# A hybrid decoder trunk on one core: the MLP's last blocks in another order, and fewer mean matmuls at the end

## The chip, the cores and the metric

The kernel runs on one core of one Trainium2 chip, in one launch. The metric is the device time of that core in microseconds; the time before is the median of three runs.

## The reference

The program is a decoder trunk of four layers over 256 positions with 1024 features, all in float32. Each layer adds a token mixer, an MLP and a per-layer input embedding to the residual h; a norm ends the trunk. The mixers are a state-space layer (layers 0 and 3), forgetting attention (layer 1) and gated linear attention (layer 2). The change touches the MLP of all four layers and the final norm.

```python
def rmsnorm(x, g):
    y = x * rsqrt(mean(x * x, axis=-1) + 1e-6)
    return y * g

def sqrelu_mlp(xn, w1, w2):                 # w1: 1024 x 4096, w2: 4096 x 1024
    return square(relu(xn @ w1)) @ w2

for i in range(4):
    h = h + mixer_i(rmsnorm(h, norm_mix[i]))
    h = h + sqrelu_mlp(rmsnorm(h, norm_mlp[i]), mlp_w1[i], mlp_w2[i])
    h = h + (p[i] @ ple_proj[i]) * sigmoid(rmsnorm(h, norm_ple[i]) @ ple_gate[i])
return rmsnorm(h, final_norm)
```

## The kernel before

h lies in SBUF transposed, as eight tiles of 128 features x 256 positions (`H[k]`, in pairs `HH[n]`). Most weight products are done in split precision: a weight unit (256 rows x 512 columns, 512 KB) is loaded by the sync engine (L153, tile `raw`), rounded on ScalarE to its high part (L157, `whi`), and VectorE computes the remainder (L159, `wlo`). There are 3 buffers of `raw` and 4 each of `whi` and `wlo`, so units are made ready a few ahead of TensorE, and a buffer is free again when TensorE has done the last matmul that reads it. Activations have a high and a low part too, side by side.

The MLP is a sequence of steps, written out by hand in the string `MLP`. The 4096 hidden features are eight blocks of 512, 0 to 7.

- `fC` is the first product of block C: four weight units, each with 16 matmuls (`wide`, L209 and L211: for each of four output banks two of 512 columns with `whi` and two of 256 columns with `wlo`), 64 matmuls in all. Its evacuation (`summed`, L219 and L220: a copy on ScalarE and an add on VectorE for each bank, then the squared relu at L387 and a split at L267 and L268) makes the activation `s[C]`. A bank is free after its L220.
- `sCB` is the second product, from block C to half B of the outputs: two weight units, 32 matmuls. Four blocks accumulate in the same banks; after block 3 and after block 7 the sum `y` is evacuated (L219, L220), scaled (L406) and added to h (L408). For blocks 4 to 7 and half 1 a narrower form with two banks is used.

PSUM has eight banks in four tags: `acc` (3), `wk` (3), `po` (1), `mk` (1). `fC` uses three `wk` and `mk`, or three `acc` and `mk` for C = 4 and 5. `sC0` uses three `acc` and `po`; `sC1` three `wk` and `po` for blocks 0 to 3, and two `wk` for blocks 4 to 7. So in the part of the sequence that the change touches, s31 ends the sum y in `wk` and `po`, s40 begins a sum in `acc` and `po`, and f6 and f7 both use `wk` and `mk`.

Between the steps, after steps 1 to 15 of the sequence (counted from 0), `further()` runs one side step of a generator, `s5_ahead`, which prepares tables for layer 3's state-space mixer during the MLPs of layers 0 to 2. A side step's instructions are put behind the last weight load, the last `wlo` and the last matmul issued so far, each on its own engine. The fourteenth side step is a small table through the `mk` bank in layer 0 (L832 to L840), some small VectorE and ScalarE operations and loads in layer 1 (`bb`, `bc`, L708 to L710, L913, L914), and empty in layer 2; the fifteenth is empty in layer 0, a VectorE product of two factors in layer 1 (`rot`) and 34 small matmuls into `mk` in layer 2 (L922 to L927).

The final stage squares the eight tiles of h on ScalarE (L1167), sums each over the features by a matmul with a column of 1/1024 as the moving operand, for each half of the positions (L1169, into `ms`), and turns h to rows by matmuls with the gains on a diagonal (`turn`, L1163, into four banks). Each of these float32 matmuls shows as two instructions in the profile. The inverse root of the mean (L341 on VectorE, L345 on GpSimd) then scales the rows on VectorE (L1181) and ScalarE (L1183), and the sync engine writes them out (L1184). The last gate of layer 3 (L476 to L479) produces the last four tiles of h one by one.

The order of instructions on each engine is set ahead of time by a planner: it simulates the engines' time and takes, on each engine, the first instruction in program order that it holds to be ready. `issue_after(x)` puts the block's instructions on x's engine behind x. At run time each engine keeps the order that it was given.

Of the kernel before, what the change touches and what calls it, by code (L numbers as in the profile page):

```python
# [12 lines left out]
AF = mybir.ActivationFunctionType  # L13
ALU = mybir.AluOpType
# [15 lines left out]

MLP = "f0 f1 f2 s00 f3 s10 s20 s30 s01 s11 f4 s21 f5 s31 s40 f6 f7 s50 s60 s70 s41 s51 s61 s71"


def _turn():
# [22 lines left out]
class Trunk:  # L59
# [312 lines left out]
    def mlp(self, l):  # L372
# [41 lines left out]

        for i, step in enumerate(MLP.split()):
            c = int(step[1])
# [733 lines left out]
    def final(self, out):  # L1150
        nc = self.nc
        gain = self.t4("gain", (128, 8, 128))
        for k in range(8):
            nc.gpsimd.tensor_scalar(gain[:, k], self.ident, self.gains[:, 3 * DEPTH, k:k + 1], None, ALU.mult)
        ms = self.psum((128, 2))

        hT = [[self.psum((128, 4, 128), tag) for tag in tags] for tags in (("acc", "acc"), ("po", "mk"))]
        sq = [self.t4("sq", (128, 4, T), tag="c4") for _ in range(2)]
        halves = [slice(half * 128, (half + 1) * 128) for half in range(2)]

        def turn(k):
            for half, t in enumerate(halves):
                nc.tensor.matmul(hT[k // 4][half][:, k % 4], self.H[k][:, t], gain[:, k], start=True, stop=True)  # L1163

        for k in range(8):
            s = sq[k // 4][:, k % 4]
            nc.scalar.activation(s, self.H[k], AF.Square)  # L1167
            for half, t in enumerate(halves):
                last = nc.tensor.matmul(ms[:, half:half + 1], s[:, t], self.mean, start=k == half == 0, stop=k == 7, skip_group_check=True)  # L1169
            if k < 6:  # L1170
                turn(k)
        with self.tc.issue_after(last.ins):
            turn(6)
            turn(7)
        r = self.inverse_root(ms)
        for half in range(2):
            o = self.t4("fin", (128, 2, 512))
            for c in range(2):
                v, ps = o[:, c], hT[c][half].rearrange("t k f -> t (k f)")
                if c == 0:  # L1180
                    nc.vector.tensor_scalar(v, ps, r[:, half:half + 1], None, ALU.mult)  # L1181
                else:
                    nc.scalar.activation(v, ps, AF.Identity, scale=r[:, half:half + 1])  # L1183
            nc.sync.dma_start(out[half * 128:(half + 1) * 128, :], o.rearrange("t c f -> t (c f)"))  # L1184
# [62 lines left out]
```

## Time and profile before

| | |
|---|---|
| time, median of 3 runs | 1460.38 us (1458.03 to 1461.11) |
| profiled execution: time / span | 1461.99 us / 1460.2 us |
| TensorE (PE) busy | 1403.9 us, 96% |
| weight loads of TensorE (PEld) busy | 1266.9 us, 87% |
| VectorE (DVE) busy | 1054.3 us, 72% |
| ScalarE (ACT) busy | 723.2 us, 50% |
| GpSimd (POOL) busy | 86.8 us, 6% |
| mean granted TensorE clock | 0.984 |
| HBM read and written | 242.68 MB and 7.86 MB, 172 GB/s over the span |

A row of the timeline gives the start and length in us, the engine, the line of the kernel, the operation, output <- inputs, the shapes and how often it follows itself; in brackets stands how long the engine was idle before, and what ended that. A row of the waits gives an engine's operation, what it waited for, the sum in us, how often, and the longest. A row of the windows gives, for a stretch of the span, the busy time of each engine with the count of instructions, the granted clock (1.00 is full speed), the DMA engines' share and GB/s. Lengths of matmuls are modelled and overlap; their starts show the pace.

### The profile page before, as it was taken

Reading aid. Unit: us, or ns where it says so; the run is one execution under the profiler, and the core shown is the slowest. Engines: PE = TensorE matmul, PEld = TensorE weight load, DVE = VectorE, ACT = ScalarE, POOL = GpSimd, SP = SyncE. Lnnn points to the kernel's source line nnn. Section 1 sums busy time; section 2 is a strip of 40 time slices with the busy share of each in tenths; the row PEclk is TensorE's granted clock in tenths of the full one; section 3 lists DMA queues with packets and bytes.
Section 4 is the critical chain, followed back from the end, with each engine's and each line's share of the span. In section 5 each row is a group of like instructions: output and inputs, shape, how many; then the busy total and the mean of one; then the engine's idle time right before and its main releaser. Section 6 shows DMA issues by size and latency. Waiting matters only on the chain. (4 is left out here: it accounts for less than half of the span.)

```text
span 1460.2 us, 26622 instructions
## 1 busy us (share of the span) xinstructions
PE 1403.9 (96%) x10734; PEld 1266.9 (87%) x10734; DVE 1054.3 (72%) x1739; ACT 723.2 (50%) x1118; POOL 86.8 (6%) x142
## 2 busy tenths in 40 slices
PE   7889999999999999999999999999997899999998
PEld 6779988889999888888989588888997899888898
DVE  8994578767776578887676468886777946766665
ACT  3233565445655654545566455454563345545443
POOL 3100000010000000010004000100000000000020
PEclk9999999999999999999999999999999899999999
DMA  6623555566554347775555446774665446566551
GB/s 211 198 81 119 186 176 189 187 203 191 175 151 142 108 153 236 230 228 180 188 164 157 132 129 190 234 229 150 222 246 152 137 141 185 179 188 187 173 191 69
DMA packets 146347, 255.06 MB, mean 175 GB/s; under 512 B 24768, under 2 KB 35296, under 8 KB 146224
## 3 DMA queue, kind: packets, MB, share of 16 engines
q1 hardware_dynamic: 132912, 234.35, 50.8%
q0 software_dynamic: 5248, 17.31, 3.7%
q10 hardware_dynamic: 8064, 1.71, 0.6%
q8 instruction: 84, 1.38, 0.4%
q14 instruction: 39, 0.32, 0.1%
HBM read 242.68 MB, written 7.86 MB: 172 GB/s over the span
## 5 line engine op out<-in xcount | busy, mean ns | idle before, releaser
L159 DVE TENSOR_TENSOR wlo<-raw,whi 128x1024 fp32r<-128x1024 f32 x406 | 494.2, 1226 | 289.0 <-ACT whi L157 283.9
L157 ACT CAST whi<-raw 128x1024 fp32r<-128x1024 f32 x406 | 422.5, 1049 | 453.4 <-PE mk L209 77.7
L209 PE MATMUL wk<-x,whi 128*128 128x512 f32 x576 | 182.4, 401 | 7.5 <-DVE relu L220 7.5
L211 PEld LDWEIGHTS wk<-x,wlo 128*128 128x128 f32 x576 | 106.8, 190 | 23.1 <-issue 0.2
L209 PE MATMUL acc<-s,whi 128*128 128x512 f32 x384 | 118.5, 395 | 0.0
L211 PE MATMUL wk<-x,wlo 128*128 128x256 f32 x576 | 113.3, 281 | 0.0
L173 PE MATMUL acc<-x,whi 128*128 128x256 f32 x352 | 99.8, 288 | 4.6 <-DVE u L1060 2.9
L209 PEld LDWEIGHTS wk<-x,whi 128*128 128x128 f32 x576 | 92.2, 192 | 11.5 <-DVE relu L220 8.6
L174 PE MATMUL acc<-x,whi 128*128 128x256 f32 x352 | 100.3, 287 | 0.0
L175 PE MATMUL acc<-x,wlo 128*128 128x256 f32 x352 | 100.1, 286 | 0.0
L211 PEld LDWEIGHTS acc<-s,wlo 128*128 128x128 f32 x384 | 70.3, 188 | 15.8
L209 PE MATMUL mk<-x,whi 128*128 128x512 f32 x256 | 81.5, 395 | 0.0
L211 PE MATMUL acc<-s,wlo 128*128 128x256 f32 x384 | 74.3, 280 | 0.0
L173 PEld LDWEIGHTS acc<-x,whi 128*128 128x128 f32 x352 | 67.6, 194 | 6.4 <-issue 4.1
L175 PE MATMUL wk<-s,wlo 128*128 128x256 f32 x256 | 72.4, 283 | 0.0
L174 PE MATMUL wk<-s,whi 128*128 128x256 f32 x256 | 72.4, 283 | 0.0
L173 PE MATMUL wk<-s,whi 128*128 128x256 f32 x256 | 72.4, 283 | 0.0
L175 PEld LDWEIGHTS acc<-x,wlo 128*128 128x128 f32 x352 | 68.1, 194 | 0.1
L174 PEld LDWEIGHTS acc<-x,whi 128*128 128x128 f32 x352 | 68.0, 194 | 0.2
L209 PEld LDWEIGHTS acc<-s,whi 128*128 128x128 f32 x384 | 59.6, 189 | 1.4
L209 PE MATMUL po<-s,whi 128*128 128x512 f32 x192 | 60.7, 396 | 0.0
L209 PE MATMUL wk<-s,whi 128*128 128x512 f32 x192 | 60.1, 395 | 0.0
(399 smaller groups left out, 3376.0 us busy)
## 6 DMA issues: line engine op xcount, KB each, us to landing
raw<-mlp_w SPq DMA_DIRECT2D x256, 512.0 KB, 4.3
raw<-s_w_glu SPq DMA_DIRECT2D x32, 512.0 KB, 3.6
raw<-ple_gate SPq DMA_DIRECT2D x32, 512.0 KB, 3.6
raw<-fox_w_in SPq DMA_DIRECT2D x24, 512.0 KB, 3.8
raw<-gla_w_in SPq DMA_DIRECT2D x24, 512.0 KB, 3.6
raw<-s_w_out SPq DMA_DIRECT2D x16, 512.0 KB, 4.2
kept<-kept SPq DMA_DIRECT2D x12, 512.0 KB, 4.4
raw<-s_w_in SPq DMA_DIRECT2D x11, 512.0 KB, 4.7
```

Of the source, the lines that this page charges most:

```text
L157: nc.scalar.copy(hi, raw)
L159: self.last_lo = nc.vector.tensor_tensor(lo, raw, hi.bitcast(F32), ALU.subtract)
L173: mm(ps, hi, x[:, 0], start=first, stop=False, skip_group_check=True)
L174: mm(ps, hi, x[:, 1], start=False, stop=False, skip_group_check=True)
L175: self.last_mm = mm(ps, lo, x[:, 0], start=False, stop=last, skip_group_check=True)
L209: mm(ps[n], hi[:, i, s], v[i], start=first and i == 0, stop=False, skip_group_check=True)
L211: self.last_mm = mm(ps[n][:, 0], lo[:, i, s], v[i][:, 0], start=False, stop=last and i == UK - 1, skip_group_check=True)
```

## The change

In the MLP's sequence, f6 comes ahead of s40 instead of behind it. In the final stage, the squares of tiles 0 to 3 are added in pairs by one VectorE operation (tiles 0 and 1 with 2 and 3), so that two means instead of four are taken of them; the means of tiles 4 and 5 come behind those, their turns behind their means; the means of tiles 6 and 7 come behind the means of 4 and 5, and their turns behind their means. The means of the first four tiles and their turns are put behind the last matmul of the gate.

```diff
-MLP = "f0 f1 f2 s00 f3 s10 s20 s30 s01 s11 f4 s21 f5 s31 s40 f6 f7 s50 s60 s70 s41 s51 s61 s71"
+MLP = "f0 f1 f2 s00 f3 s10 s20 s30 s01 s11 f4 s21 f5 s31 f6 s40 f7 s50 s60 s70 s41 s51 s61 s71"
...
-        for k in range(8):
-            s = sq[k // 4][:, k % 4]
-            nc.scalar.activation(s, self.H[k], AF.Square)
+        def mean(x, first, last):
             for half, t in enumerate(halves):
-                last = nc.tensor.matmul(ms[:, half:half + 1], s[:, t], self.mean, start=k == half == 0, stop=k == 7, skip_group_check=True)
-            if k < 6:
+                self.last_mm = nc.tensor.matmul(ms[:, half:half + 1], x[:, t], self.mean, start=first and half == 0, stop=last, skip_group_check=True)
+
+        for k in range(4):
+            nc.scalar.activation(sq[0][:, k], self.H[k], AF.Square)
+        nc.vector.tensor_tensor(sq[0][:, 0:2], sq[0][:, 0:2], sq[0][:, 2:4], ALU.add)
+        with self.tc.issue_after(self.last_mm.ins):
+            for k in range(2):
+                mean(sq[0][:, k], k == 0, False)
+            for k in range(4):
                 turn(k)
-        with self.tc.issue_after(last.ins):
-            turn(6)
-            turn(7)
+        for k in range(4, 8):
+            nc.scalar.activation(sq[1][:, k - 4], self.H[k], AF.Square)
+        for k in range(4, 8, 2):
+            with self.tc.issue_after(self.last_mm.ins):
+                for i in range(2):
+                    mean(sq[1][:, k + i - 4], False, k + i == 7)
+            with self.tc.issue_after(self.last_mm.ins):
+                for i in range(2):
+                    turn(k + i)
```

## The prediction

> **What bounds the kernel now.** I read the page's busy times first, then TensorE's waits, then the timeline at the longest of them, then the windows with the granted clock, and last the chain of waits at the end.
>
> ```profile
> PE 1403.9 (96%) x10734; PEld 1266.9 (87%) x10734; DVE 1054.3 (72%) x1739; ACT 723.2 (50%) x1118; POOL 86.8 (6%) x142
> ```
> ```profile
> PE wk L209 <- DVE relu L220: 7.5, 6, 1.9
> ```
> ```profile
> 321.28 0.73 PE L209 MATMUL wk<-x,whi 128*128 128x512 f32 x2 [1.77 <-DVE relu L220]
> 659.76 0.73 PE L209 MATMUL wk<-x,whi 128*128 128x512 f32 x2 [1.94 <-DVE relu L220]
> 1007.58 0.73 PE L209 MATMUL wk<-x,whi 128*128 128x512 f32 x2 [1.20 <-DVE relu L220]
> 1371.17 0.73 PE L209 MATMUL wk<-x,whi 128*128 128x512 f32 x2 [1.39 <-DVE relu L220]
> ```
>
> TensorE is busy for 96%, so only its gaps can be won, or work taken off it. Its longest wait in sum is a first-product matmul waiting for L220, the VectorE add that frees a PSUM bank. Four of the six, 1.77 + 1.94 + 1.20 + 1.39 = 6.30 us, are one place, once in each layer: f7 starting directly behind f6 in the same banks (three wk and mk). The other two, 1.2 us, lie elsewhere in the MLPs and stay; they are what is late next.
>
> ```profile
> 1369.43 0.92 ACT L219 COPY relu<-wk 128x256 f32<-128x256 f32 x3
> ```
> ```profile
> 1369.55 1.23 DVE L159 TENSOR_TENSOR wlo<-raw,whi 128x1024 fp32r<-128x1024 f32 x1 [1.45 <-PE mk L209]
> 1370.70 1.08 DVE L220 TENSOR_TENSOR relu<-wk,relu 128x256 f32<-128x256 f32 x3
> ```
>
> In layer 3, f6's results leave PSUM only behind a weight remainder on VectorE: copied from 1369.43, the first add starts at 1370.70, and f7 at 1371.17.
>
> ```profile
> 319.30:322.67 3.37, 1.60 (x10) 1.22 (x10) 3.00 (x6) 2.48 (x6) 0.50 (x1) 1.00 0.91 208
> 322.67:326.08 3.41, 3.41 (x13) 2.92 (x12) 3.09 (x5) 1.22 (x2) 0.00 (x0) 0.50 1.03 327
> 321.28:334.10 12.82, 12.82 (x64) 11.15 (x65) 8.61 (x13) 6.44 (x9) 0.00 (x0) 0.87 0.73 234
> 657.20:660.59 3.39, 1.45 (x9) 1.12 (x8) 2.92 (x6) 2.95 (x6) 0.00 (x0) 1.00 0.47 171
> 660.59:664.00 3.41, 3.41 (x13) 2.83 (x12) 3.38 (x6) 1.24 (x2) 0.00 (x0) 0.50 0.69 206
> 659.76:672.60 12.84, 12.84 (x65) 11.11 (x66) 9.12 (x13) 5.60 (x10) 0.00 (x0) 0.87 0.38 123
> 1371.17:1382.45 11.28, 11.28 (x65) 9.86 (x65) 7.77 (x11) 5.49 (x10) 0.00 (x0) 1.00 0.37 107
> 1004.30:1007.71 3.41, 2.21 (x13) 1.75 (x13) 2.19 (x4) 2.83 (x6) 0.00 (x0) 1.00 0.66 232
> 513.82:517.23 3.41, 1.62 (x17) 1.14 (x16) 1.36 (x2) 2.12 (x3) 0.00 (x0) 1.00 0.57 186
> 517.23:520.64 3.41, 3.41 (x17) 3.41 (x18) 0.56 (x2) 0.00 (x0) 0.00 (x0) 0.50 0.55 157
> ```
>
> Columns: stretch, length, busy time of PE, PEld, DVE, ACT, POOL, then the granted clock. After the two longest waits the clock stands at 0.50 for 3.41 us. The 64 matmuls of f7 then take 12.82 and 12.84 us (layers 0 and 1) against 11.28 in layer 3 at full clock: 1.54 + 1.56 = 3.10 us more. Stretches with PE busy 1.60, 1.45 and 1.62 of 3.4 us are followed by half clock, the one with 2.21 is not.
>
> **The change, edit 1: f6 ahead of s40.** Nothing is added or removed. s40 moves with all it issues behind f6: two weight loads on SP, two casts on ScalarE, two remainders on VectorE, 32 matmuls. f6 has four of each, 64 matmuls and its evacuation (4 copies, 4 adds, 2 squares, 2 splits). POOL's order changes only through the side steps below.
>
> What goes: f7 now starts behind s40, which uses acc and po. f6's evacuation has s40's 32 matmuls to hide under. The same pattern is in the trace already, f4 then s21 then f5:
>
> ```profile
> 284.50:288.50 4.00, 4.00 (x25) 3.52 (x24) 3.96 (x10) 1.68 (x2) 0.00 (x0) 1.00 0.68 214
> 1335.20:1339.20 4.00, 4.00 (x25) 3.47 (x25) 2.40 (x3) 1.37 (x3) 0.00 (x0) 1.00 0.69 219
> ```
>
> These windows hold the start of f5 in layers 0 and 3; TensorE is busy throughout. So I take -6.30 for the waits, and -3.10 for the slow clock that they bring.
>
> What comes: f6 now starts directly behind s31, in the three wk banks that s31's y holds. Every matmul of f6, s40 and f7 is queued behind that wait on TensorE. Its price is read from the moment s40 starts today (the acc row), which is when f6 would start, and the wk adds of y:
>
> ```profile
> 302.06 0.63 PE L209 MATMUL acc<-s,whi 128*128 128x512 f32 x2
> 640.94 0.63 PE L209 MATMUL acc<-s,whi 128*128 128x512 f32 x2
> 989.50 0.62 PE L209 MATMUL acc<-s,whi 128*128 128x512 f32 x2
> 1352.89 0.63 PE L209 MATMUL acc<-s,whi 128*128 128x512 f32 x2
> 1359.86 0.63 PE L209 MATMUL po<-s,whi 128*128 128x512 f32 x2
> ```
> ```profile
> 302.45 0.75 DVE L220 TENSOR_TENSOR y<-wk,y 128x256 f32<-128x256 f32 x2
> 639.82 0.28 DVE L708 TENSOR_TENSOR bb<-bc,coef 128x128 f32<-128x128 f32 x1
> 642.50 0.41 DVE L220 TENSOR_TENSOR y<-wk,y 128x256 f32<-128x256 f32 x1
> 644.44 0.74 DVE L220 TENSOR_TENSOR y<-wk,y 128x256 f32<-128x256 f32 x2
> 990.30 0.42 DVE L220 TENSOR_TENSOR y<-wk,y 128x256 f32<-128x256 f32 x1
> 1353.27 0.75 DVE L220 TENSOR_TENSOR y<-wk,y 128x256 f32<-128x256 f32 x2
> ```
>
> A bank's share of one weight unit takes 11.28/16 = 0.70 us, so the third wk bank is needed 1.41 us after the start. In layers 0, 2 and 3 the last wk add ends 1.14, 1.22 and 1.13 us after it: wait 0 to 0.2 us each. In layer 1 it ends 4.24 us after it (645.18), because the side step's small VectorE operations (bb, from 639.82) and f5's evacuation stand between; mk is free early and fills 0.70 us or more. That bounds layer 1 at 4.24 - 1.41 = 2.8 us as it stands. But this side step is the fourteenth, called after f6 now instead of s40, so its operations go behind f6's last remainder, two units later, and leave that place: I take 1.0. Sum of new waits 0.2 + 1.0 + 0 + 0.1 = 1.3 us; bounds 0 and 4 x 2.8 = 11.2.
>
> There is one further relief: today s40's po matmuls wait for y's po bank until 1359.86, and hold their weight buffers so long. Behind f6 that bank is long free. I count nothing for it, as TensorE had other work.
>
> The side steps keep their count. In layer 0 the table (3 matmuls, one copy, POOL's transfers) goes behind f6, in layer 1 the fetch, in layer 2 the last 34 small matmuls go behind s40. All are read a layer later at the earliest, so the cost is nothing; if TensorE met the mk bank unready there, the price is a wait like 1.20.
>
> **Edit 2: the final stage.**
>
> ```profile
> 1446.98 0.34 PE wk L1169 x4
> 1452.34 0.80 PE wk L1169 x8
> 1453.17 0.17 DVE rrow L341
> ```
> ```profile
> 1440.22 1.34 ACT L1167 ACTIVATE sq<-h 128x256 f32<-128x256 f32 x4 [1.36 <-DVE h L479]
> 1449.62 0.75 ACT L1167 ACTIVATE sq<-h 128x256 f32<-128x256 f32 x2 [0.59 <-DVE h L479]
> ```
> ```profile
> 1445.58 0.76 DVE L476 TENSOR_TENSOR z<-wk,rstd 128x256 f32<-128x256 f32 x2 [4.79 <-PE wk L175]
> ```
> ```profile
> L310 DVE TENSOR_TENSOR sq<-sq 128x512 f32<-128x512 f32 x3 | 2.0, 683 | 0.0
> ```
>
> Between the last gate matmul and the sum rrow, TensorE works without a gap on 32 mean instructions (two to a matmul) and 24 turns. The added squares make 8 of the 32 needless, at 0.34/4 to 0.80/8, 0.085 to 0.10 us each: -0.7 us. The order of the turns gives nothing more: six tiles' turns stay ahead of the last means by program order, two stay behind as today, under the inverse root. The last squares end at 1450.37, before the last means could start (about 1451.6), so ScalarE does not bind. The add is one VectorE operation like L310's, 0.68 us; its squares end at 1441.56 and VectorE is idle for 4.79 us before 1445.58, so it costs nothing. Queued behind it on VectorE are the z and h operations of the last four tiles; put by the planner among them, it would delay the last h by up to 0.68 and eat the gain.
>
> **Sum.** -6.30 - 3.10 + 1.3 - 0.7 = -8.8 us. The profiled execution took 1461.99 us (span 1460.2): 1453.2. It stands 1.6 above the median of the runs, 1460.38. A wait of 1.8 us brings the slow clock only where it falls into one stretch of 3.4 us, and the stretches lie on a grid (322.67, 517.23 and 660.59 are whole multiples of 3.41 apart) whose place will differ by run; so a median run probably has one slow stretch of 1.55 fewer to lose, and ends at the same 1453.2.
>
> [...]
>
> **The rivals.**
> - *The waits go, the slow clock stays* (its stretches have another cause, or neighbouring short idles keep it): 1461.99 - 5.7 = 1456.3. For it: 517.23 has one without any f7. Against: each follows a stretch under half busy. Chance 0.12.
> - *The wait only moves*: f6 behind s31 waits as f7 behind f6 did, 6.30 in sum, with none to two slow stretches. For it: it is the same reuse of banks, and layer 1's rows. Against: y leaves bank by bank, in time in three layers. 1461.99 - 0.7 - (0 to 3.10) = 1458.2 to 1461.3. Chance 0.18, half of it with at most one slow stretch, under 1459.8.
> - *Slower*: with y unevacuated in the planner's view, VectorE work is put ahead of its adds in every layer as in layer 1. Four waits of 2.8 = 11.2 with four slow stretches of 1.55 = 6.2, less 10.1 saved: +7.3, 1469.3. It decides from about 1.8 us a layer (7.2 + 6.2 against 10.1, +3.3). Chance 0.10.
>
> **How the numbers follow.** The forecast case has 0.60, with its own range 1450 (no new wait and 0.9 in the final stage give 1451.7; half the spread of the runs shown, 1.5, lies below) to 1456 (4 us of waits). The range 1450.0 to 1459.8 adds the first rival and half of the second: 0.81. About 0.2%, 2.9 us, is what a measurement of this kernel can tell from no change. Faster: 0.60 + 0.12 and a little of the second, 0.73; same 0.17; slower 0.10.
>
> **What would show it.** Right: no L220 wait of over 1 us at f7's first matmul, TensorE busy through s40's start, no half clock within f7, 24 mean instructions ending about 0.7 us sooner after the last gate matmul. Wrong: a wait for y's L220 at f6's first wk matmul of over 1.5 us, in layer 1 first; half clock within f6; the squares' add behind a z operation.

## The result, and the profile after

The changed kernel takes 1448.84 us (median of 6 runs, 1446.57 to 1449.71), the kernel before on the same chip 1459.61 (6 runs, 1456.45 to 1462.32): ratio 0.9925, 95% interval 0.991 to 0.994. That is 10.8 us less. The forecast had the sign and the place right, but not the size: 1453.2 was 7.2 below the median shown, and the result lies 1.2 under the low end of the range, 1450.0. The profiled execution of the changed kernel took 1446.57 us, its span 1444.5, at a mean clock of 0.991 (0.984 before).

First the busy times of the changed kernel, to be held against those of before (1403.9 for PE):

```profile
PE 1396.0 (97%) x10726; PEld 1259.8 (87%) x10726; DVE 1054.5 (73%) x1740; ACT 723.6 (50%) x1118; POOL 86.9 (6%) x142
```

Eight PE instructions fewer and one more on VectorE: the final stage. The span fell by 15.7 in this pair, more than the medians did. Next TensorE's waits (sum, times, longest, us):

```profile
PE wk L321 <- DVE relu L220: 1.2, 2, 0.7
PE wk L209 <- DVE relu L220: 1.0, 2, 0.8
...
PE mk L209 <- DVE relu L220: 0.5, 1, 0.5
```

The line that led the list before (7.5 us, six times) is down to the two waits that the prediction said would stay. One new line has come, for `mk`. The windows over f7 in layers 0, 1 and 3 (length, busy PE, PEld, DVE, ACT, POOL, granted clock, DMA share, GB/s; in layer 0, where three matmuls of the side step run inside f7, its last 0.6 us lie outside):

```profile
315.35:326.50 11.15, 11.15 (x66) 9.41 (x65) 6.02 (x7) 5.33 (x8) 3.79 (x7) 1.00 0.59 191
649.88:661.05 11.17, 11.17 (x67) 9.75 (x66) 8.84 (x11) 6.40 (x9) 0.00 (x0) 1.00 0.64 188
1356.48:1367.63 11.15, 11.15 (x66) 9.73 (x65) 6.50 (x8) 5.26 (x9) 0.00 (x0) 1.00 0.69 213
```

No gap, full clock, where layers 0 and 1 took 12.82 and 12.84 before. Now the place that the prediction feared, f6's start behind s31. The timeline of TensorE in layer 1, and then in layer 3:

```profile
632.13 0.39 PE L211 MATMUL po<-s,wlo 128*128 128x256 f32 x2
633.04 0.74 PE L209 MATMUL mk<-x,whi 128*128 128x512 f32 x2 [0.53 <-DVE relu L220]
633.63 0.40 PE L211 MATMUL mk<-x,wlo 128*128 128x256 f32 x2
633.86 0.63 PE L209 MATMUL mk<-x,whi 128*128 128x512 f32 x2
...
1339.52 0.40 PE L211 MATMUL po<-s,wlo 128*128 128x256 f32 x2
1339.75 0.63 PE L209 MATMUL mk<-x,whi 128*128 128x512 f32 x2
...
1340.45 0.62 PE L209 MATMUL mk<-x,whi 128*128 128x512 f32 x2
...
1341.84 0.63 PE L209 MATMUL wk<-x,whi 128*128 128x512 f32 x2
```

f6 does not begin with `wk` at all. The planner, which held y's banks to be not yet free, put f6's `mk` matmuls of three weight units first, 1341.84 - 1339.75 = 2.1 us of work, and `wk` only then. The one wait left, 0.53 us in layer 1, is for f5's result in `mk` (relu), not for y. Layers 0, 2 and 3 have none.

That y itself leaves its banks hardly sooner than before is seen on VectorE in layer 1:

```profile
632.57 0.42 DVE L220 TENSOR_TENSOR relu<-mk,relu 128x256 f32<-128x256 f32 x1
632.91 1.22 DVE L159 TENSOR_TENSOR wlo<-raw,whi 128x1024 fp32r<-128x1024 f32 x1
634.04 0.42 DVE L220 TENSOR_TENSOR y<-wk,y 128x256 f32<-128x256 f32 x1
634.37 0.68 DVE L387 SCALAR_TENSOR_TENSOR relu<-relu 128x512 f32<-128x512 f32 x1
634.97 0.69 DVE L268 TENSOR_TENSOR s<-relu,s 128x512 fp32r<-128x512 f32 x1
635.58 0.75 DVE L220 TENSOR_TENSOR y<-wk,y 128x256 f32<-128x256 f32 x2
```

The last `wk` add of y ends 4.2 us after s31's last pair of matmuls began (635.58 + 0.75 against 632.13). In before it was 645.18 - 640.71 = 4.5 us. What stands between is a weight remainder (L159) and f5's evacuation (L387, L268); the side step's operations come later, from 637.37 on.

The final stage, from the timeline of VectorE and then from the chain that ended last:

```profile
1426.78 0.69 DVE L1171 TENSOR_TENSOR sq<-sq 128x512 f32<-128x512 f32 x1 [0.80 <-ACT sq L1170]
1430.78 0.76 DVE L476 TENSOR_TENSOR z<-wk,rstd 128x256 f32<-128x256 f32 x2 [3.31 <-PE wk L175]
```
```profile
1432.18 0.79 PE wk L1167 x8
1432.97 1.89 PE acc L1163 x16
1434.86 0.79 PE wk L1167 x8
...
1436.65 0.80 PE wk L1167 x8
...
1437.47 0.17 DVE rrow L341
```

The add of the squares ran in VectorE's idle time, 4.0 us ahead of the first z. From the first mean to rrow the chain takes 1437.47 - 1432.18 = 5.29 us, against 1453.17 - 1446.98 = 6.19 before: 0.90 less. The chain of before goes back and forth between four mean instructions and four turns:

```profile
1446.98 0.34 PE wk L1169 x4
1447.32 0.55 PE acc L1163 x4
1447.87 0.34 PE wk L1169 x4
```

Summed over the pieces of each chain, the means take 2.95 us before and 2.38 after, 0.57 less, and the same 24 turns 3.19 and 2.88, 0.31 less.

Where the MLPs' time went is seen without the luck of the other stages in the length of each MLP from behind f2 on: from its L355 matmul to the first matmul of the next norm (L321). In the table, worked out from the starts of these rows, e1, e2, e4 and e8 are runs told of below.

| layer | before | e4 (before again) | e2 (final only) | after | e1 (MLP only) | e8 (after again) |
|---|---|---|---|---|---|---|
| 0 | 155.94 | 154.20 | 154.31 | 152.39 | 152.39 | 152.39 |
| 1 | 160.40 | 161.00 | 160.64 | 157.46 | 157.91 | 157.86 |
| 2 | 164.29 | 164.43 | 164.78 | 162.84 | 162.84 | 162.84 |
| 3 | 153.43 | 153.47 | 153.35 | 151.77 | 151.77 | 151.77 |
| sum | 634.06 | 633.10 | 633.08 | 624.46 | 624.91 | 624.86 |

The change takes 9.6 us out of the MLPs in the profiled pair and 8.2 to 8.6 against the other executions of the old order. With 0.9 in the final stage that is 9.1 to 10.5 us. The rest of the 15.7 between the two spans lies outside these stretches, where the code is the same: one slow stretch of the clock, in a mixer, stood at 517.23 in before (and at 513.34 in e4) and none there in after, and waits there differ by run: those of L1007 for P sum to 7.1 us in before, 7.8 in e4 and 5.3 in after.

### The profile page after: what moved, and what is told of

It is laid out like the page before. It is cut to its first block, busy times and chain, and to the rows that moved or that the text cites. A ratio compares the mean times of both kernels' runs of the same rounds, so it can differ in the third digit from the quotient of the medians.

```text
span 1444.5 us, 26608 instructions
## 1 busy us (share of the span) xinstructions
PE 1396.0 (97%) x10726; PEld 1259.8 (87%) x10726; DVE 1054.5 (73%) x1740; ACT 723.6 (50%) x1118; POOL 86.9 (6%) x142
## 3 DMA queue, kind: packets, MB, share of 16 engines
q10 hardware_dynamic: 8064, 1.71, 0.6%
## 5 line engine op out<-in xcount | busy, mean ns | idle before, releaser
L159 DVE TENSOR_TENSOR wlo<-raw,whi 128x1024 fp32r<-128x1024 f32 x406 | 494.7, 1226 | 288.4 <-ACT whi L157 281.8
L209 PE MATMUL wk<-x,whi 128*128 128x512 f32 x576 | 181.3, 396 | 1.0 <-DVE relu L220 1.0
L211 PEld LDWEIGHTS wk<-x,wlo 128*128 128x128 f32 x576 | 106.6, 188 | 23.4
L209 PE MATMUL acc<-s,whi 128*128 128x512 f32 x384 | 120.1, 396 | 0.0
L211 PE MATMUL wk<-x,wlo 128*128 128x256 f32 x576 | 113.1, 279 | 0.0
L209 PEld LDWEIGHTS wk<-x,whi 128*128 128x128 f32 x576 | 90.0, 189 | 3.5 <-DVE relu L220 1.3
L211 PEld LDWEIGHTS acc<-s,wlo 128*128 128x128 f32 x384 | 71.6, 188 | 16.6
L209 PE MATMUL mk<-x,whi 128*128 128x512 f32 x256 | 81.6, 396 | 0.5 <-DVE relu L220 0.5
L211 PE MATMUL acc<-s,wlo 128*128 128x256 f32 x384 | 75.6, 279 | 0.0
L209 PE MATMUL po<-s,whi 128*128 128x512 f32 x192 | 60.6, 396 | 0.0
L209 PE MATMUL wk<-s,whi 128*128 128x512 f32 x192 | 60.1, 395 | 0.0
L209 PEld LDWEIGHTS acc<-s,whi 128*128 128x128 f32 x384 | 59.1, 189 | 0.6
```

Of the source, the lines that this page charges most:

```text
L159: self.last_lo = nc.vector.tensor_tensor(lo, raw, hi.bitcast(F32), ALU.subtract)
L209: mm(ps[n], hi[:, i, s], v[i], start=first and i == 0, stop=False, skip_group_check=True)
L211: self.last_mm = mm(ps[n][:, 0], lo[:, i, s], v[i][:, 0], start=False, stop=last and i == UK - 1, skip_group_check=True)
```

## The experiments

**e1 and e2: each edit alone.** e1 has only the new order of the MLP, e2 only the new final stage.

```diff
 e1
-MLP = "... f5 s31 s40 f6 f7 s50 ..."
+MLP = "... f5 s31 f6 s40 f7 s50 ..."
 e2
 (the final stage of the change, MLP as before)
```

> Only the MLP's order is changed (f6 ahead of s40); the final stage is as before. Theory A (the MLP's order carries nearly the whole gain, and the two slow-clock stretches behind f7's start are in every run of before): 9.6 us less, as the MLPs of the two traces differ, of which 6.3 are f7's waits, 3.1 the slow clock, 0.5 given back at f6's start. Rival B (as the prediction had it: a median run has but one of the two stretches): 6.5 to 8 us less, and the rest of the 10.8 measured lies in the final stage or in chance.

> Only the final stage is changed; the MLP's order is as before. Both theories: 24 mean instructions instead of 32, the sum rrow 0.9 us sooner after the last gate matmul (0.7 predicted), time 0.9 us less, which is within what can be told from no change. Rival B leaves room for up to 3 us here; then rrow would come 2 to 3 us sooner.

e1: 1448.55 us against 1458.78 for before (29 runs), ratio 0.9944 (0.9923 to 0.9966), so 5.0 to 11.2 us less. The time can't choose between the 9.6 of theory A and the 6.5 to 8 of rival B. By the table the order of the MLP is worth 8.2 to 9.2 us, nearly all of the gain; f7's four waits are gone, and f6 waits once:

```profile
633.82 0.73 PE L209 MATMUL mk<-x,whi 128*128 128x512 f32 x2 [0.59 <-DVE relu L220]
```

e2: 1457.95 us, ratio 0.9994 (0.9982 to 1.0007). The time alone can't tell 0.9 us from nothing; the traces do. From the start of the first mean in the timeline to rrow, the four versions with the old final stage (before, e1, e3, e4) take 6.35 us each, and the six with the new one (after, e2, e5 to e8) 5.45 or 5.46.

**e3: the wait filled.** To tell the slow clock from the wait itself, a float32 matmul with zero weights is put between f6 and f7 in the old order, adding zero to s40's bank. It does not touch the bank that f7 waits for.

```diff
             first(c)
+                if c == 6:
+                    with self.tc.issue_after(self.last_mm.ins):
+                        nc.tensor.matmul(y[0][:, 0], self.far[:, 0:128], self.H[0], start=False, stop=False, skip_group_check=True)
```

> The kernel before, with one float32 matmul of zero weights (two instructions, some 0.84 us by the lines of the first state-space product) added into s40's open bank behind f6 in each layer, so that TensorE works for part of f7's wait; the order of the MLP is as before. Theory A (the slow clock follows a stretch of 3.4 us that is less than half busy): the banks come free when they did, the idle time at f7 shrinks by 0.84 to 0.4 to 1.1 us a layer, no half clock stands in f7 of layers 0 and 1, f7 takes 11.3 us there, and the kernel is about 3.1 us faster (1.6 if only one stretch is in a median run). Rival C (the slow clock has another cause): half clock in f7 as before, time the same within 0.5 us.

1460.11 us, ratio 1.0011 (0.9996 to 1.0027): no gain, so neither expectation came in as written. No half clock stands in any MLP of this run. In layer 1, TensorE's timeline and the windows on the clock's own grid:

```profile
654.04 0.60 PE L421 MATMUL acc<-h,far 128*128 128x256 f32 x2
...
656.70 0.50 PE L209 MATMUL wk<-x,whi 128*128 128x512 f32 x1 [2.07 <-DVE relu L220]
```
```profile
652.83:656.24 3.41, 1.80 (x11) 1.27 (x9) 2.38 (x3) 3.23 (x6) 0.00 (x0) 1.00 0.41 150
656.24:659.65 3.41, 2.95 (x16) 2.55 (x17) 3.38 (x8) 1.43 (x3) 0.00 (x0) 1.00 0.95 284
```

The filler covered only about 0.4 us, and behind it f7 waited as before: 1.60, 2.07, 1.87 and 0.77 us in the four layers, 6.3 in sum. From the start of f6's last matmul to that of f7's first it is 9.2 us, summed over the layers, against 7.4, 8.0 and 7.9 in before, e2 and e4. So the bank came later, by 1.2 to 1.8 us in sum, which is about what was filled; why was not looked into. As a test of the clock's price by the time it is inconclusive, because the old order has about one slow stretch in an MLP to lose (next run), not two.

**e4: the kernel before, once more.** A second profile of the same code shows what of the prediction's first rows was that one execution.

> The kernel before once more, for its trace and for how far two sets of runs of one kernel differ. Theory A: half clock stands again behind f7's start in layers 0 and 1 (waits 1.8 and 1.9), ratio 1.000. Rival B: in one of the two layers only, since the place of the 3.4 us stretches differs by run.

1458.49 us, ratio 0.9992 (0.9978 to 1.0005). f7's waits on the timeline, and the windows at the one in layer 1:

```profile
318.37 0.73 PE L209 MATMUL wk<-x,whi 128*128 128x512 f32 x2 [1.57 <-DVE relu L220]
655.72 0.73 PE L209 MATMUL wk<-x,whi 128*128 128x512 f32 x2 [2.48 <-DVE relu L220]
1003.32 0.74 PE L209 MATMUL wk<-x,whi 128*128 128x512 f32 x2 [1.32 <-DVE relu L220]
1367.18 0.73 PE L209 MATMUL wk<-x,whi 128*128 128x512 f32 x2 [1.43 <-DVE relu L220]
```
```profile
653.29:656.70 3.41, 0.98 (x5) 0.89 (x6) 3.20 (x6) 2.83 (x6) 0.00 (x0) 1.00 0.47 141
656.70:660.11 3.41, 3.41 (x11) 2.84 (x11) 3.38 (x6) 1.24 (x2) 0.00 (x0) 0.50 0.69 205
```

The waits sum to 6.80 us here (6.30 in the first profile, 6.84 in e2), and one slow stretch follows, in layer 1 alone, as rival B had it; e2 has one there too, the first profile had two.

**e5 and e6: why f6 hardly waits behind s31.** Two causes are on offer. The prediction's: the fourteenth side step, whose small VectorE operations hold up y in layer 1, moves behind f6. The rival's: the planner begins f6 with `mk`, which covers y's way out of `wk`. e5 puts the side step back ahead of f6; e6 keeps the changed kernel's order of steps but forces each unit's `mk` matmuls behind its `wk` ones in f6.

```diff
 e5
-            if i and i < 16:
-                further()
+            for _ in range({"s31": 2, "f6": 0}.get(step, 1)):
+                if i and i < 16:
+                    further()
 e6, in wide(), strict for f6
-            for i in range(UK):
-                mm(ps[n], hi[:, i, s], ...)
+            with self.tc.issue_after(self.last_mm.ins) if strict and n == 3 else nullcontext():
+                for i in range(UK):
+                    mm(ps[n], hi[:, i, s], ...)
 ...
```

> The changed kernel, but the fourteenth side step is called before f6 (behind s31) instead of behind it. Theory A (the prediction's step: in layer 1 this step's small VectorE operations stood ahead of y's wk adds, and their leaving made the new wait short): with them back, the wk adds of layer 1 end again some 4 us after s31, and the idle time at f6's start in layer 1 is 1.5 to 2.8 us instead of 0.53; time 1 to 2 us more, not to be told from no change. Rival D (the planner's three units of mk matmuls ahead of the wk ones hide y's evacuation, wherever the side step stands): idle 0.5 to 0.8 us there, time the same.

> The changed kernel, but in f6 the matmuls into mk are put behind the wk ones of the same weight unit, so that none of them can go first. Theory A (y leaves its wk banks in time, as the rows of before have it): idle at f6's first wk matmul 0 to 0.3 us in layers 0, 2 and 3 and up to 1 in layer 1, time the same within 1 us. Rival D (the mk matmuls hid the wait, 2.1 us of them): idle of 1 us or more in each layer, 4 to 6 us slower, with slow clock perhaps in layer 1.

e5: 1446.92 us, ratio 0.9928 (0.9912 to 0.9944). The timeline of layer 1, with the side step's operation (L711) ahead of y's adds:

```profile
632.72 0.39 PE L211 MATMUL po<-s,wlo 128*128 128x256 f32 x2
632.86 0.28 DVE L711 TENSOR_TENSOR bc<-bc 128x128 f32<-128x128 f32 x1
632.95 0.63 PE L209 MATMUL mk<-x,whi 128*128 128x512 f32 x2
...
634.19 0.42 DVE L220 TENSOR_TENSOR y<-wk,y 128x256 f32<-128x256 f32 x1
...
635.12 0.75 DVE L220 TENSOR_TENSOR y<-wk,y 128x256 f32<-128x256 f32 x2
...
635.51 0.62 PE L209 MATMUL wk<-x,whi 128*128 128x512 f32 x2
```

No wait at all, less than either theory had: y's last `wk` add ends at 635.87, 2.9 us behind f6's start, but TensorE has `mk` until 635.51 and needs the third `wk` bank only 1.4 us after that. The test is weaker than it was meant to be, because most of the side step's operations ran from 626.27 on, ahead of s31's end, and L711 alone (0.28 us) stands at y's adds. With the changed kernel beside it the answer is still plain. From the start of s31's last pair to the end of y's last `wk` add it is 3.2 us with the side step early (e5), 4.2 and 3.7 with it late (after, e8) and 4.5 before. So the side step was not what held y in layer 1.

e6: 1448.95 us, ratio 0.9942 (0.992 to 0.9963), 2.8 us over the changed kernel measured beside it (e8, below); the two intervals overlap. Its timeline and windows in layer 1 (its lines are numbered one higher):

```profile
631.93 0.39 PE L212 MATMUL po<-s,wlo 128*128 128x256 f32 x2
...
634.68 0.42 DVE L221 TENSOR_TENSOR y<-wk,y 128x256 f32<-128x256 f32 x1
635.15 1.19 PE L210 MATMUL wk<-x,whi 128*128 128x512 f32 x2 [2.83 <-DVE y L221]
...
636.21 0.75 DVE L221 TENSOR_TENSOR y<-wk,y 128x256 f32<-128x256 f32 x2
```
```profile
631.80:635.21 3.41, 0.58 (x5) 0.34 (x3) 3.41 (x6) 3.20 (x6) 0.00 (x0) 1.00 0.76 260
635.21:638.62 3.41, 3.41 (x10) 2.91 (x11) 3.41 (x8) 1.12 (x3) 0.00 (x0) 0.50 0.65 210
```

Without the planner's choice, the feared wait is there: 2.83 us for y in layer 1, none in layers 0, 2 and 3, with a slow stretch behind it. That layer's MLP takes 161.27 us against 157.86 in e8. So in layer 1 the planner's choice hides the wait, while in the other three there was none to hide, and neither expectation held in full. That 2.83 is also the prediction's bound for layer 1 is partly luck: the bound was counted for the third `wk` bank, and this wait ended with y's first add (634.68 + 0.42), which came later here, 3.2 us after s31's last pair began, against 2.2 in the trace of before.

**e7: an attempt at a better version.** The waits left at the MLPs' starts (L321 and L209, 2.2 us together) come from f0 to f2 following each other in `wk` and `mk`; e7 gives f1 the `acc` banks.

```diff
-            ps = self.banks([("wk", "acc")[c in (4, 5)]] * 3 + ["mk"])
+            ps = self.banks([("wk", "acc")[c in (1, 4, 5)]] * 3 + ["mk"])
```

> The changed kernel, and f1 uses the acc banks, so that f0, f1 and f2 no longer follow each other in the same ones. The waits left at the MLPs' start are 0.72 and 0.52 (the mean behind f1) and 0.28 and 0.76 (f1, f2), 2.3 us of idle time. Theory A: they go, 2.3 to 3.3 us less than the changed kernel, 12 to 13 less than before. Rival: s00, which needs acc, waits for f1's evacuation instead, or f1 for the bank of the product before the MLP; then the time is that of the changed kernel.

1447.97 us, ratio 0.9935 (0.9919 to 0.9951): no better than the changed kernel, and theory A's 2.3 to 3.3 us did not come. The waits for L220 in `wk` at the starts went, but in layer 1 it waits for s (as e8 does, 0.7) and at f6:

```profile
580.24 0.73 PE L209 MATMUL acc<-s,whi 128*128 128x512 f32 x2 [0.68 <-DVE s L268]
634.36 0.74 PE L209 MATMUL mk<-x,whi 128*128 128x512 f32 x2 [0.77 <-DVE relu L220]
```

**e8: the changed kernel, once more**, measured beside e5 to e7.

> The changed kernel once more, for its trace and as the measure for e5 to e7 on the same chip. Theory A: 10 us less than before; no half clock from s31 to the end of f7 in any layer; idle time at f6's start in layer 1 alone, 0.4 to 0.7.

1446.17 us against 1457.53 for before (11 runs), ratio 0.9923 (0.9908 to 0.9938), 11.4 us. Its timeline marks no wait at f6's start in any layer, where 0.4 to 0.7 was expected in layer 1; in layer 1, where s31's last row (po, L211) ends at 632.69:

```profile
632.72 0.73 PE L209 MATMUL mk<-x,whi 128*128 128x512 f32 x2
```

No version run here is told apart from the changed kernel as faster.

## Why the prediction was right in kind and short in size

The sum for a median run, 8.8 less one slow stretch of 1.55, gave 7.2 us. The terms that were too small add 2.4 to it: 0.8 at f6, 0.9 for the price of a wait, which the sum put at nothing, 0.5 for larger waits at f7 and 0.2 in the final stage.

- **The waits at f7, -6.30: right.** All four are gone. They were somewhat low for this kernel: 6.80 and 6.84 in two other executions.
- **The slow clock at f7, -3.10 for the profiled execution: right there.** No MLP of after, e1, e5 or e8 has half clock at f7. So the first rival, "the waits go, the slow clock stays", fell. In layer 1, e6's gap of 2.83 and e4's of 2.48 us were followed by half clock (0.50 in the windows above).
- **The new waits at f6, +1.3: the term that was mis-sized.** Measured 0.53 in after, 0.59 in e1, none marked in e5 and e8. The step behind it failed in three places. First, the 1.0 for layer 1 was taken because the side step leaves that place; it left, and y's last `wk` add still came 4.2 us after s31's last pair began, against 4.5 before. Second, "`mk` is free early and fills 0.70 us or more" was wrong both ways in layer 1: `mk` was what f6 waited for, and the planner drew the `mk` work of three units forward, 2.1 us, not one unit's. Third, the bound of 2.8 was counted for the third bank alone. In the trace of before the second is free at 644.85, 3.9 us after the start, and would be needed 0.70 after it, which makes 3.2. Forbidding the planner's choice brings 2.83 back in layer 1 (e6), and none in the layers that had 0 to 0.2. The second rival, "the wait only moves", and the slower one fell for the same reason: with y still in its banks the planner found other work for TensorE.
- **The price of a wait: understated, by the way it was read.** In the rows of layer 3 above, a matmul without a wait starts at 1339.75, 0.17 us before the modelled end of the one ahead (1339.52 + 0.40); idle time counts only from that end. And the first four matmuls behind a wait are slower: 633.04 to 633.86 is 0.82 us, 1339.75 to 1340.45 is 0.70. So by these rows I estimate that a wait costs 0.17 + 0.12, some 0.3 us, more than its bracket says. The table bears it out where the clock plays no part: layers 2 and 3 gain 1.45 and 1.66 us for waits of 1.20 and 1.39. For the three waits that went net of the one that came it is about 0.9 us. In the profiled pair -6.30 - 3.10 + 0.53 - 0.9 = -9.8 stands against a measured 634.06 - 624.46 = 9.6.
- **The final stage, -0.7: nearly right, -0.90 measured.** 24 mean instructions in three groups, the add hidden. The means gave 0.57. The other 0.31 of the chain's pieces lies in the turns, which now follow each other in two groups in place of five; the prediction had said that their order gives nothing more.
- **Turning the sum into a median: a step that hid the gain.** The prediction noted that its profile stood 1.6 above the median, that a median run has one slow stretch fewer, and that both end at 1453.2. So for a median run it forecast only 7.2. e4 and e2 have the one stretch in the MLPs. But such a run has larger waits (6.8): 6.8 + 1.55 + 0.9 for the price of the waits, less 0.5 at f6, plus 0.9 at the end is 9.7. That is inside the intervals of the result (8.8 to 13.1 us by its ratio) and of e8, whose middles, 10.8 and 11.4, are one to two us more. The granted clocks of the runs point to where that rest may lie. Span times what the clock lacks of full speed is 19.6 us on average in the 11 runs of before beside e8, and 16.4 in e8's six: 3.2 less, where the sum has 1.55. The same figure is 3.7 less for e5, but 1.5 for e6 and 0.5 for e7, and only the profiled execution shows in which stage, so how much of it belongs to the change stays open. The medians of before themselves lie at 1459.61, 1458.78 and 1457.53, under the 1460.38 of the three runs from which the 7.2 is counted.

## What to carry to other kernels

When two stages that reuse the same PSUM banks are moved apart, price the new neighbours bank by bank: here it counted how much work in an already free bank the planner could draw ahead, and not only when the last bank came free. Read a wait's cost from the starts of the matmuls around it against the undisturbed pace, because the bracket of idle time left a few tenths out here (some 0.3 us by the estimate above). And profile the old kernel a second time before summing its waits and slow stretches, since both changed here from one execution to the next (waits at f7 of 6.30, 6.80 and 6.84 us, two slow stretches behind them in one execution and one in the others).

## What the runs showed of the hardware

The prediction had four stretches to go by: 1.60, 1.45 and 1.62 us of work with half clock behind them, 2.21 without. The ten traces (before, after, e1 to e8) give more. In each, the stretches at a granted clock of 0.50 began whole multiples of 3.413 us apart. I cut each trace by its own grid and added up TensorE's matmul rows in every stretch at full clock, from 20 us on, up to about 3 us before the end. Of the 56 stretches with TensorE busy for less than half (under 1.71 us), 53 were followed by half clock; of the 4017 others, 5 were. In before alone it was 10 of 10 and none of 398, in after 5 of 5 and 1 of 404. That is a count of this kernel's traces, with the line at half a stretch drawn by me. e4's stretch with 0.98 us fell on one side and e3's with 1.80 on the other, and a gap of 2.07 us in e3, lying across the end of a stretch, cost nothing of the clock.

Why eight stretches went against it is not settled. The five busier ones, with 1.76 to 2.52 us, hold matmuls of few columns, whose lengths in the profile are modelled: 64x64 in four traces, at 31.6 to 32.1 us, and the means (128x1) in e8, at 203.6. Three more like the latter lie behind the means of the final stage in e1, e6 and e7, in the last few us that the count leaves out. For the three idler ones, with 1.50 to 1.67 us, no reason was found.
